# The last mixed pair of each chunk: three sums of weights on GpSimd in place of VectorE

## The chip, the cores and the metric

The kernel runs on one core of one Trainium2 chip. The metric is the device time of one execution in microseconds (us). Five engines share the core's on-chip memory: TensorE (PE in the rows, PEld for its weight loads), VectorE (DVE), ScalarE (ACT), GpSimd (POOL) and SyncE (SP), which issues the DMAs.

## The reference

One layer of an encoder, for 256 rows of width 2048, all in float32. Cut to what matters here:

```python
def swiglu(h, w_gate, w_up, w_down):
    return (jax.nn.silu(h @ w_gate) * (h @ w_up)) @ w_down

x = x + 0.5 * swiglu(rmsnorm(x, ffn1_norm), ffn1_w_gate, ffn1_w_up, ffn1_w_down)
...   # attention and linear attention, output product, cross attention on a memory
x = x + 0.5 * swiglu(rmsnorm(x, ffn2_norm), ffn2_w_gate, ffn2_w_up, ffn2_w_down)
```

The two SwiGLU stages (FFN 1 at the start, FFN 2 at the end) have weights of 2048x5632 (twice) and 5632x2048. They are the stages that the change touches.

## The kernel before, in words

**Split weights.** Every float32 weight tile is split in two on its way to TensorE: ScalarE rounds it to `wh` (a cast, L128), and VectorE computes the rest `wl` = weight minus `wh` (a subtraction, L129). Both are made in `parts`. A product is three matmuls: `wh` by the high part of the activations, `wl` by the same high part, and `wh` by the low part. `hth` and `htl` are the split activations of the first two products, `acth`/`actl` those of the third.

**Chunks.** An FFN runs in chunks. One call of `pair_gemm` is one chunk: for 512 columns of the gate and 512 of the up weight (11 chunks an FFN, c0 to c10), or for 1024 columns of the down weight (two calls after each group of 4, 4 and 3 chunks). So an FFN has 17 calls, and the kernel 34. A chunk goes over pairs of 128-row blocks of the weights, 8 pairs a chunk (6 in the last two down calls). A pair is one unit of the loop at L248 onward: DMA of a raw tile of 128x2048 (`raw`, 3 buffers), split, matmuls into four accumulators (`acc`).

**Plain and mixed pairs.** A plain pair has 24 matmuls of 512 columns. A mixed pair takes the 2x2 blocks of weights and activations by a scheme of seven products in place of eight, so it has 21 matmuls, but it wants four sums of weight blocks: `mixed_parts` (L203) makes t1 and t3 in one operation of 1024 columns (L208), then t2 (L213) and t4 (L214) of 512 columns each, into `wsum`, which has one buffer. t2 reads t1, and t4 reads t2. Then it splits three of the four raw blocks (1536 columns) and the four sums (2048 columns), each into a buffer of `wh` and one of `wl`; there are 4 buffers of each (`wspl`). Four of the seven products go into extra banks (`bank`), which `middle` (L302, L303) adds up after the last mixed pair.

**Order.** Pairs are taken in ORDER8 = (1, 0, 3, 2, 5, 4, 6, 7), with 1, 3 and 5 mixed, so that mixed and plain alternate; c0 of each FFN takes them in ORDER_FIRST = (0, 2, 4, 6, 1, 3, 5, 7), with the three mixed ones in a row. The 6-pair chunks take (1, 0, 3, 2, 4, 5) with 1 and 3 mixed. So a chunk's last mixed pair is pair 5, or pair 3 of six. Kernels of this kind give their operations in program order, and the framework's planner sets each engine's own queue when the program is built: at each moment of its own model it takes the operation that is ready and came first. On the chip each queue is then strictly in order. `issue_after(summed.ins)` tells the planner that the VectorE operations of the block (the two subtractions of L129) stand behind t4 in VectorE's queue.

**One mixed pair on the engines before:** VectorE makes the three sums, then the `wl` of the raw blocks; ScalarE casts the sums as soon as they and a buffer are there; then VectorE makes the `wl` of the sums. TensorE begins a mixed pair with the raw block B11 (three matmuls) and takes t1 next, `wh` first, then `wl`.

**GpSimd before** has a few small operations (the reciprocal square roots of L92 and L94 on 2 to 8 columns, constants) and the descriptors of some small DMAs of `setup_mix` (L436, L479 to L491).

Of the kernel before, what the change touches and what calls it, by code (L numbers as in the profile page):

```python
# [15 lines left out]
ALU = mybir.AluOpType  # L16
# [44 lines left out]
class Kernel:  # L61
# [138 lines left out]
            dma(raw[:, :, CW:], wb, cb, CW)  # L200
        return flat[:, :nk * 2 * CW]

    def mixed_parts(self, raw):  # L203
        nc = self.nc
        q = [raw[:, i * CW:(i + 1) * CW] for i in range(4)]
        t = self.wsum.tile([P, 4 * CW], F32, name="wsum")
        t1, t3, t2, t4 = (t[:, i * CW:(i + 1) * CW] for i in range(4))
        nc.vector.tensor_tensor(  # L208
            out=t[:, :2 * CW].rearrange("p (j n) -> p j n", j=2),
            in0=raw[:, CW:3 * CW].rearrange("p (j n) -> p j n", j=2),  # L210
            in1=q[0].unsqueeze(1).broadcast_to([P, 2, CW]), op=ALU.add,
        )
        nc.vector.tensor_tensor(out=t2, in0=t1, in1=q[2], op=ALU.add)  # L213
        summed = nc.vector.tensor_tensor(out=t4, in0=t2, in1=q[3], op=ALU.add)  # L214
        forms = {}
        with self.tc.issue_after(summed.ins):
            for src, names in ((raw[:, CW:], ("B11", "B22", "B21")), (t, ("t1", "t3", "t2", "t4"))):
                wh, wl = self.parts(src, 4 * CW)
                for i, name in enumerate(names):
                    forms[name] = tuple(w[:, i * CW:(i + 1) * CW] for w in (wh, wl))  # L220
        return forms

    def pair_gemm(self, xs, cols, k0, order, middle, ahead=None):

        nc = self.nc
        out = [[self.acc.tile([P, CW], F32, name="acc") for _ in range(2)] for _ in range(NB)]
        if ahead:
            ahead(0)  # L230

        units = []
        for p in order:
            units += [(p, (0,)), (p, (1,))] if ahead and not units else [(p, (0, 1))]
        mixed = [i for i, (p, _) in enumerate(units) if xs[p][0]]
        extra, seen = {}, set()
        side = self.pending
        self.pending = []

        def product(key, bank, high, part, stop):  # L240
            self.last_pe = nc.tensor.matmul(out=bank, lhsT=high, rhs=part, start=key not in seen, stop=stop)  # L241
            seen.add(key)

        def step(u):
            if side and not (mixed and mixed[0] <= u < mixed[-1]):
                side.pop(0)()

        for u, (p, kk) in enumerate(units):  # L248
            if ahead and u:
                ahead(u)  # L250
            last = u == len(units) - 1
            is_mixed, xh, xl = xs[p]
            with ExitStack() as first:
                if ahead and not u:
                    for ins in self.first:
                        first.enter_context(self.tc.issue_after(ins))
                raw = self.raw_pair(cols, k0 + 2 * p + kk[0], len(kk))
                if is_mixed:
                    forms = self.mixed_parts(raw)
                else:  # L260
                    wh, wl = self.parts(raw, 4 * CW)
            if is_mixed:
                if u == mixed[0]:
                    extra = {name: self.bank() for name in ("p1", "p5", "p7", "p6")}
                for name, i, form in self.MIXED:
                    key = self.PLACE.get(name, name)
                    bank = extra[name] if name in extra else out[key[0]][key[1]]
                    fh, fl = forms[form]
                    ah, al = (t[:, i * P:(i + 1) * P] for t in (xh, xl))
                    stop = u == mixed[-1] if name in extra else last  # L270
                    product(key, bank, ah, fh, False)
                    product(key, bank, ah, fl, False)
                    product(key, bank, al, fh, stop)
                if u == mixed[-1]:
                    middle(extra)
                    step(u)
                continue
            x = lambda t, k, b: t[:, (2 * k + b) * P:(2 * k + b + 1) * P]
            w = lambda t, k, c: t[:, (2 * (k - kk[0]) + c) * CW:(2 * (k - kk[0]) + c + 1) * CW]
            if last:  # L280

                turns = [(k, b, (c,)) for c in range(2) for b in range(NB) for k in kk]
            else:
                turns = [(k, b, (0, 1)) for k in kk for b in range(NB)]
            for t, (k, b, cs) in enumerate(turns):
                for c in cs:
                    product((b, c), out[b][c], x(xh, k, b), w(wh, k, c), False)
                    product((b, c), out[b][c], x(xh, k, b), w(wl, k, c), False)
                for c in cs:
                    product((b, c), out[b][c], x(xl, k, b), w(wh, k, c), last and k == kk[-1])  # L290
                if not last and b == NB - 1:
                    step(u)
        for piece in side:
            piece()
        return out

    def middle(self, extra):

        nc = self.nc
        p1, u3 = (self.sums.tile([P, CW], F32, name="su", bufs=4) for _ in range(2))  # L300
        u4, v = (self.sums.tile([P, CW], F32, name="sg", bufs=2) for _ in range(2))
        add = lambda out, a, b: nc.vector.tensor_tensor(out=out, in0=a, in1=b, op=ALU.add)  # L302
        nc.scalar.copy(out=p1, in_=extra["p1"])  # L303
        add(u4, extra["p6"], p1)
        add(u3, extra["p7"], u4)
        add(v, extra["p5"], u3)
        add(u4, extra["p5"], u4)
        return p1, u4, u3, v
# [897 lines left out]
```

## Time and profile before

| | |
|---|---|
| time, median of 3 runs | 1893.19 us (1891.2 to 1893.41) |
| profiled execution | 1893.06 us, of which the span of the trace 1891.4 us |
| mean granted TensorE clock | 0.995 |
| busy in the span | PE 98%, VectorE 82%, ScalarE 54%, GpSimd 3% |
| DMA | 56.2% of 16 engines' time, 187 GB/s read |

How to read it: a row of the timeline gives the start in us from the start of the span, the duration in us, engine, line, operation, what it writes and reads, the shapes, and in brackets the idle time of the engine before it with what ended that. A busy PE is not PE at its peak, since the ends of matmuls are modelled; the distance of the starts of two matmuls is what one costs (0.23 us for 512 columns at the full clock).

### The profile page before, as it was taken

How to read it: one execution, taken by the hardware profiler on the slowest of the kernel's cores; microseconds unless marked ns; L12 is line 12 of the kernel's file. 1: busy time of each engine (PE TensorE's matmuls, PEld its weight loads, DVE VectorE, ACT ScalarE, POOL GpSimd, SP SyncE). 2: the span in 40 equal slices, each digit the busy share in tenths (PEclk: the TensorE clock that was granted, in tenths of full speed). 3: DMA queues.
4: the chain of work that ended last, by engine and by line, in shares of the span. 5: the costliest groups of instructions: out<-in, count | busy, mean ns of one | idle time of the engine just before them, and what ended most of it. 6: DMA issues, size and time to landing. Idle time of an engine off the chain costs nothing.

```text
span 1891.4 us, 21793 instructions
## 1 busy us (share of the span) xinstructions
PE 1862.5 (98%) x8418; PEld 1529.6 (81%) x8418; DVE 1556.6 (82%) x1691; ACT 1017.2 (54%) x1088; POOL 60.7 (3%) x114
## 2 busy tenths in 40 slices
PE   8899999999999999999999999999999999999999
PEld 6688888888888888788778878778888888888887
DVE  7899999998999996555565645999998899999897
ACT  6555545555545554664555655655544555545552
POOL 1000000000000100120100020000000000000000
PEclk9899999999999999999999999999999999999999
DMA  7565556665566555544436553566556665556653
GB/s 247 178 201 200 183 200 213 193 205 198 201 212 201 188 183 178 174 156 146 133 133 210 178 169 133 178 200 200 201 197 204 204 198 200 199 200 201 200 200 134
DMA packets 148072, 356.01 MB, mean 188 GB/s; under 512 B 11018, under 2 KB 11120, under 8 KB 147968
## 3 DMA queue, kind: packets, MB, share of 16 engines
q1 hardware_dynamic: 147360, 354.07, 56.2%
q8 instruction: 66, 1.08, 0.2%
q0 software_dynamic: 608, 0.55, 0.2%
q14 instruction: 38, 0.31, 0.0%
HBM read 352.48 MB, written 2.10 MB: 187 GB/s over the span
## 4 chain that ended last, share of the span: by engine, by line
PE 92%; DVE 3%; ACT 3%; issue 1%; DMA 1%; POOL 0%; SPq 0%; ACTq 0%; DVEq 0%
PE acc L241 55%; PE acc L142 18%; PE bank L241 14%; PE bank L350 2%; ACT wh L128 1%; DVE wl L129 1%; ACT junk L384 1%; DMA raw<-in_ffn_w_up_dram 1%; DVE wsum L208 0%; PE bank L949 0%; PE bank L804 0%; PE bank L785 0%; PE bank L948 0%; PE bank L1003 0%; PE bank L1012 0%
## 5 line engine op out<-in xcount | busy, mean ns | idle before, releaser
L129 DVE TENSOR_TENSOR wl<-raw,wh 128x2048 fp32r<-128x2048 f32 (+4 forms) x405 | 716.4, 1771 | 192.1 <-ACT wh L128 190.9
L128 ACT CAST wh<-raw 128x2048 fp32r<-128x2048 f32 (+4 forms) x405 | 601.7, 1494 | 405.8 <-PE acc L241 172.0
L241 PE MATMUL acc<-wh,hth 128*128 128x512 f32 x1078 | 423.4, 395 | 4.2 <-ACT wh L128 4.2
L241 PE MATMUL acc<-wl,hth 128*128 128x512 f32 x1078 | 420.3, 390 | 0.8 <-DVE wl L129 0.8
L241 PE MATMUL acc<-wh,htl 128*128 128x512 f32 x1078 | 363.2, 390 | 0.0
L128 ACT CAST wh<-wsum 128x2048 fp32r<-128x2048 f32 x98 | 187.6, 1914 | 256.7 <-DVE wsum L214 182.5
L129 DVE TENSOR_TENSOR wl<-wsum,wh 128x2048 fp32r<-128x2048 f32 x98 | 224.5, 2291 | 39.6 <-ACT wh L128 39.6
L241 PEld LDWEIGHTS acc<-wh,hth 128*128 128x128 f32 x1078 | 203.4, 189 | 46.1 <-ACT wh L128 4.8
L241 PEld LDWEIGHTS acc<-wh,htl 128*128 128x128 f32 x1078 | 202.9, 188 | 42.9
L241 PEld LDWEIGHTS acc<-wl,hth 128*128 128x128 f32 x1078 | 203.0, 188 | 42.5 <-DVE wl L129 1.4
L241 PE MATMUL acc<-wh,actph 128*128 128x512 f32 x448 | 176.0, 393 | 0.0
L241 PE MATMUL acc<-wl,actph 128*128 128x512 f32 x448 | 174.4, 389 | 0.0
L241 PE MATMUL acc<-wh,actpl 128*128 128x512 f32 x448 | 145.6, 389 | 0.0
L208 DVE TENSOR_TENSOR wsum<-raw 128x1024 f32<-128x1024 f32 x98 | 119.5, 1219 | 3.8 <-DMA raw<-in_ffn_w_up_dram 2.2
L142 PE MATMUL acc<-wh,hth 128*128 128x512 f32 (+1 forms) x288 | 113.2, 395 | 0.0
L241 PE MATMUL bank<-wl,hth 128*128 128x512 f32 x264 | 105.8, 401 | 7.3 <-DVE wl L129 7.3
L142 PE MATMUL acc<-wl,hth 128*128 128x512 f32 (+1 forms) x288 | 109.9, 383 | 0.0
L241 PE MATMUL bank<-wh,hth 128*128 128x512 f32 x264 | 102.5, 396 | 3.6 <-ACT wh L128 3.6
L241 PE MATMUL bank<-wh,htl 128*128 128x512 f32 x264 | 104.4, 396 | 0.0
L241 PEld LDWEIGHTS acc<-wh,actpl 128*128 128x128 f32 x448 | 84.0, 188 | 17.9
L241 PEld LDWEIGHTS acc<-wh,actph 128*128 128x128 f32 x448 | 84.1, 188 | 17.1
L241 PEld LDWEIGHTS acc<-wl,actph 128*128 128x128 f32 x448 | 84.2, 188 | 16.9
(280 smaller groups left out, 2394.4 us busy)
## 6 DMA issues: line engine op xcount, KB each, us to landing
raw<-in_ffn_w_down_dram SPq DMA_DIRECT2D x88, 1024.0 KB, 5.0
raw<-in_ffn_w_gate_dram SPq DMA_DIRECT2D x175, 512.0 KB, 3.8
raw<-in_ffn_w_up_dram SPq DMA_DIRECT2D x175, 512.0 KB, 4.6
raw<-in_w_in_dram SPq DMA_DIRECT2D x24, 1024.0 KB, 5.0
raw<-in_w_out_dram SPq DMA_DIRECT2D x16, 1024.0 KB, 5.2
raw<-in_w_in_dram SPq DMA_DIRECT2D x8, 832.0 KB, 4.6
raw<-in_mem_w_k_dram SPq DMA_DIRECT2D x4, 1024.0 KB, 5.2
raw<-in_mem_w_q_dram SPq DMA_DIRECT2D x4, 1024.0 KB, 5.2
```

The lines of the kernel that those rows point to most:

```text
L128: self.last_act = nc.scalar.copy(out=wh, in_=src)
L129: self.last_dve = nc.vector.tensor_tensor(out=wl, in0=src, in1=wh.bitcast(F32), op=ALU.subtract)
L142: self.last_pe = nc.tensor.matmul(out=out[b][c][:, :w], lhsT=high, rhs=part[:, o:o + w], start=start, stop=stop)
L208: nc.vector.tensor_tensor(out=t[:, :2 * CW].rearrange("p (j n) -> p j n", j=2), in0=raw[:, CW:3 * CW].rearrange("p (j n) -> p j n", j=2), ...
L241: self.last_pe = nc.tensor.matmul(out=bank, lhsT=high, rhs=part, start=key not in seen, stop=stop)
L350: nc.tensor.transpose(out=t[:, i * P:(i + 1) * P], in_=src(b, k), identity=self.ident)
L384: self.nc.scalar.activation(out=junk[:, :width], in_=src, func=AF.Square, accum_out=out)
```

## The change

`mixed_parts` takes the engine for the three sums as an argument. For the last mixed pair of each call of `pair_gemm` it is GpSimd, for the others VectorE as before. Where it is GpSimd, the order edge that holds VectorE's subtractions behind the sums is left out. Of 98 mixed pairs 34 are the last of their call. Sizes, buffers, casts, subtractions, matmuls and DMAs stay.

```diff
-    def mixed_parts(self, raw):
-        nc = self.nc
+    def mixed_parts(self, raw, engine):
+
...
-        nc.vector.tensor_tensor(
+        engine.tensor_tensor(
             out=t[:, :2 * CW].rearrange("p (j n) -> p j n", j=2),
             in0=raw[:, CW:3 * CW].rearrange("p (j n) -> p j n", j=2),
             in1=q[0].unsqueeze(1).broadcast_to([P, 2, CW]), op=ALU.add,
         )
-        nc.vector.tensor_tensor(out=t2, in0=t1, in1=q[2], op=ALU.add)
-        summed = nc.vector.tensor_tensor(out=t4, in0=t2, in1=q[3], op=ALU.add)
+        engine.tensor_tensor(out=t2, in0=t1, in1=q[2], op=ALU.add)
+        summed = engine.tensor_tensor(out=t4, in0=t2, in1=q[3], op=ALU.add)
         forms = {}
-        with self.tc.issue_after(summed.ins):
+        with ExitStack() as order:
+            if engine is self.nc.vector:
+                order.enter_context(self.tc.issue_after(summed.ins))
...
-                    forms = self.mixed_parts(raw)
+                    forms = self.mixed_parts(raw, nc.gpsimd if u == mixed[-1] else nc.vector)
```

## Rows read from the trace of the kernel before

**Rows 1.** The page's busy times: us, share of the span, instructions.
```profile
PE 1862.5 (98%) x8418; PEld 1529.6 (81%) x8418; DVE 1556.6 (82%) x1691; ACT 1017.2 (54%) x1088; POOL 60.7 (3%) x114
```

**Rows 2.** What PE waited for: total us, times, longest us.
```profile
PE bank L241 <- DVE wl L129: 7.3, 3, 5.1
```

**Rows 3.** Busy times by stretch: us, PE, PEld, DVE, ACT, POOL; PEclk, DMA share, GB/s.
```profile
66.00:72.00 6.00, 4.93 (x11) 3.44 (x12) 5.63 (x4) 4.36 (x3) 0.00 (x0) 0.50 0.55 175
1231.00:1236.00 5.00, 5.00 (x12) 3.50 (x12) 5.00 (x4) 2.79 (x2) 0.00 (x0) 0.50 0.61 208
347.00:390.00 43.00, 43.00 (x196) 35.56 (x195) 39.40 (x38) 23.78 (x18) 0.00 (x0) 1.00 0.62 196
```

**Rows 4.** Timeline, FFN 1's chunk c6, its last mixed pair and the pair before it.
```profile
370.93 2.29 DVE L129 TENSOR_TENSOR wl<-wsum,wh 128x2048 fp32r<-128x2048 f32 x1 [0.40 <-ACT wh L128]
373.14 2.28 DVE L129 TENSOR_TENSOR wl<-raw,wh 128x2048 fp32r<-128x2048 f32 x1
375.34 1.22 DVE L208 TENSOR_TENSOR wsum<-raw 128x1024 f32<-128x1024 f32 x1
...
377.32 0.69 DVE L214 TENSOR_TENSOR wsum<-wsum,raw 128x512 f32<-128x512 f32 x1
377.93 1.75 DVE L129 TENSOR_TENSOR wl<-raw,wh 128x1536 fp32r<-128x1536 f32 x1
380.44 2.29 DVE L129 TENSOR_TENSOR wl<-wsum,wh 128x2048 fp32r<-128x2048 f32 x1 [0.76 <-ACT wh L128]
...
375.09 1.49 ACT L128 CAST wh<-raw 128x1536 fp32r<-128x1536 f32 x1 [2.39 <-issue]
378.49 1.92 ACT L128 CAST wh<-wsum 128x2048 fp32r<-128x2048 f32 x1 [1.92 <-PE acc L241]
...
385.95 0.39 PE L241 MATMUL bank<-wl,hth 128*128 128x512 f32 x1
```

**Rows 5.** Timeline: `wl` of sums and PE's t1, FFN 1's c1 and FFN 2's c10.
```profile
85.51 2.29 DVE L129 TENSOR_TENSOR wl<-wsum,wh 128x2048 fp32r<-128x2048 f32 x1 [0.40 <-ACT wh L128]
...
90.78 0.39 PE L241 MATMUL bank<-wl,hth 128*128 128x512 f32 x1
...
1796.80 2.29 DVE L129 TENSOR_TENSOR wl<-wsum,wh 128x2048 fp32r<-128x2048 f32 x1 [0.70 <-ACT wh L128]
...
1802.32 0.39 PE L241 MATMUL bank<-wl,hth 128*128 128x512 f32 x1
```

**Rows 6.** Timeline of GpSimd and VectorE: small GpSimd operations beside a subtraction, and alone.
```profile
840.65 1.30 POOL L92 TENSOR_SCALAR sm<-sm 128x4 f32<-128x4 f32 x1
...
840.69 1.21 DVE L129 TENSOR_TENSOR wl<-raw,wh 128x1024 fp32r<-128x1024 f32 x1
...
925.50 0.19 POOL L92 TENSOR_SCALAR sm<-sm 128x4 f32<-128x4 f32 x1
```

**Rows 7.** Groups of GpSimd instructions by form: busy us, mean ns of one, idle before.
```profile
L1034 POOL MEMSET zeros<- 128x256 f32 x1 | 0.3, 322 | 24.0 <-PE acc L142 24.0
...
L468 POOL TENSOR_SCALAR_AFFINE_SELECT suffix<-suffix 128x128 f32<-128x128 f32 x1 | 0.3, 307 | 0.0
...
masks.py:197 POOL MEMSET ident<- 128x128 f32 x1 | 0.2, 204 | 0.0
```

**Rows 8.** Timeline, the last mixed pair of c0: FFN 1, then FFN 2.
```profile
50.41 2.29 DVE L129 TENSOR_TENSOR wl<-wsum,wh 128x2048 fp32r<-128x2048 f32 x1 [0.35 <-ACT wh L128]
...
54.22 0.63 PE L241 MATMUL bank<-wl,hth 128*128 128x512 f32 x1
...
1216.90 2.29 DVE L129 TENSOR_TENSOR wl<-wsum,wh 128x2048 fp32r<-128x2048 f32 x1 [0.37 <-ACT wh L128]
...
1219.25 0.50 PE L241 MATMUL bank<-wl,hth 128*128 128x512 f32 x1
```

**Rows 9.** Timeline, the last mixed pair of FFN 1's last down call.
```profile
701.45 2.29 DVE L129 TENSOR_TENSOR wl<-wsum,wh 128x2048 fp32r<-128x2048 f32 x1 [0.37 <-ACT wh L128]
...
704.09 0.39 PE L241 MATMUL bank<-wl,actmh 128*128 128x512 f32 x1
```

## Prediction: what the change will do

> **What bounds the kernel now.** I read the page's busy times first, then the waits of TensorE, then the busy times by stretch, and last the timeline of single chunks. TensorE is busy for 98% of the span [rows 1]. In a stretch of 43 us of FFN 1 it is busy all of it at the full clock, while VectorE works 39.4 us and ScalarE 23.8 [rows 3]. So the two makers of split weights have slack there, and TensorE sets the pace. What TensorE loses to them in the FFNs lies at the starts: its waits for `wl` ahead of a bank come to 7.3 us in three places, 5.1 of them in one, on the first mixed pair after FFN 1's chunk c0 [rows 2]. Behind that wait, and behind the like one in FFN 2, the granted clock is 0.50, the lower level of 1.2 GHz, for some 5 us [rows 3].
>
> So taking work off VectorE can win only at the two starts. Everywhere else the question is whether the sums on GpSimd come in time.
>
> **What is removed.** For 34 pairs VectorE drops the three sums: from 375.34 to 378.01, 2.67 us each [rows 4], 91 us in all. In the steady chunks this is worth nothing, since TensorE doesn't wait there. The order edge that falls away lets VectorE make the raw part's `wl` as soon as its cast ends (375.09 + 1.49 = 376.58, instead of 377.93 [rows 4]); TensorE wants that part only at about 385, so that is worth nothing either. DMAs: none is added. A raw buffer comes free when the last sum has read it, some 2 us later than now, and the next transfer into it starts later; that load is for a pair two pairs ahead, some 11 us of matmuls (48 at 0.23), which covers it.
>
> **What one set of sums costs on GpSimd.** No row of the trace shows a wide addition there. Nearest are a fill of 256 columns at 322 ns and of 128 at 204, so 0.92 ns for each further element, and an operation that reads and writes 128 columns at 307 ns, so 0.8 ns per element for a read on top [rows 7]; a small operation alone takes 0.19 [rows 6]. The three sums are 2048 elements in three operations. Low end: one pass of 0.92 ns carries reads and write together, 1.9 + 3 x 0.19 = 2.45 us. High end: two reads and the write in turn, 0.92 + 2 x 0.8 = 2.5 ns an element, 5.7 us. I take 4.3: the two operands read in turn with the write beside them (2 x 0.92 ns, 3.8 + 0.57), near the middle of the ends. Below nothing is excluded, since the work does not vanish.
>
> The Trainium skill has a price: its page "GPSIMD Engine Reference", section "3.1 Elementwise — side-by-side cycle accounting", gives 4497 ns for one such addition of 2048 elements. By that the set would be about 4.6 us (an estimate, with 0.1 for two more starts), and the forecast below some 8 us higher. No run here shows it.
>
> **What it waits for.** `wsum` has one buffer, so GpSimd can't begin before VectorE has read the sums of the mixed pair before: at 373.22 in the chunk shown. VectorE goes on at once, at 373.14, with the plain pair's subtraction up to 375.42 [rows 4]. Beside such subtractions (two inputs from on-chip memory) GpSimd stands still: an operation that takes 0.19 us alone took 1.30 beside one, ending at 841.95, just behind VectorE's at 841.90, though it had begun 0.04 us earlier [rows 6]. So I let GpSimd begin at 375.4, where VectorE's own sums began too. Then VectorE's subtraction of the raw part, 1.75 us, falls due at 376.58, between GpSimd's operations, and one of the two waits. Either way the sums end later by that 1.75. With 0.3 us for three starts and hand-overs:
>
> later than now by 4.3 + 1.75 + 0.3 - 2.67 = 3.7 us (1.8 at the low end of 2.45, 5.1 at the high end).
>
> The skill's page "SBUF — State Buffer", section "Who interferes with whom", has this as a lock that whoever starts first keeps for its whole instruction. The row shows GpSimd waiting although it began first, so here the trace differs in that point; by the page it would be VectorE that waits at 376.58, with the same sum.
>
> **What covers it.** Behind the sums come ScalarE's cast and VectorE's subtraction of the sums; TensorE wants that `wl` at t1, its second product. In c6 the subtraction ends at 382.73 and TensorE takes it at 385.95: 3.2 us. Besides, the cast waits now 0.4 us longer than the sums need, for a buffer (378.49 against 378.01 and 0.1 for the hand-over) [rows 4]. Room 3.6. In the first of the steady chunks it is 90.78 - 87.80 = 3.0, in the last 3.2 and another 0.3 of waiting [rows 5]; over the 28 such pairs (34 less c0 and the two 6-pair calls of each FFN) it goes from 2.4 to 4.3, half of them under 3.4. What is over is a stall of TensorE, and not given back, because VectorE's lead is bound by buffers that TensorE frees. Summed over the 28 pairs with 3.7: 24 overrun, by 11 us in all, none by more than 1.3. At 1.8 none overruns; at 5.1 all do, 48 us.
>
> Queued behind the sums on GpSimd is next to nothing in the FFNs. VectorE's queue behind the waiting subtraction of the sums holds the next plain pair's, which TensorE wants 4.8 us later than t1 (21 matmuls), so that stays covered.
>
> **The places without that room.** In c0 of each FFN three mixed pairs follow one another. Room now: 54.22 - 52.70 = 1.5 in FFN 1, and 1219.25 - 1219.19, nothing, in FFN 2 [rows 8]; overruns 2.2 and 3.6. In FFN 1's last down call 704.09 - 703.74 = 0.35 [rows 9]; 3.3. The other three 6-pair calls have over 6 us of other VectorE work between the two sets, which GpSimd can use; I put nothing there. The stalls in FFN 2's c0 and in the down call are new and long; after such a wait the clock drops as above, and 5 us at 0.50 lose 2.5 each: 5.
>
> **Sum.** 11 + 2.2 + 3.6 + 3.3 + 5 = 25 us on the profiled 1893.06 (span 1891.4 and 1.7 around it), which is 0.1 below the median of the runs. Forecast 1918. With the low end 0 + 0.3 + 1.8 + 1.5 = 4 (1897, no wait over 2 us); with the high end 48 + 3.6 + 5.0 + 4.7 + 5 = 66 (1959).
>
> **Rivals.**
>
> *The starts get shorter (faster).* VectorE is busy 5.6 of 6 us and all of 5 us in the stretches about the two start waits [rows 3], and the sums of c0's last mixed pair stand 2.67 us ahead of them in its queue. If GpSimd makes these while VectorE does the raw part and the plain pair behind, and the planner lets TensorE take that plain pair first, each start gains up to 2.67, and FFN 1's another 2 us of waiting in c0 (7.3 less 5.1 [rows 2]): 7 us, 1886. It decides where the sums end no later than those two subtractions, 1.75 + 2.28 = 4 us after the buffer is free; with 4.3 and standing still they don't. It needs the steady pairs to be covered, too.
>
> *The cover holds.* If the sums cost under 3.3 us, or GpSimd isn't held for the whole of a subtraction, the 28 pairs overrun by nothing or next to it and only the starts and the down call are left: 0 to 8 us, 1893 to 1901.
>
> *Dearer, or in another order.* At the high end of the price all pairs overrun: up to 1959. The same comes if the planner, taking GpSimd for slow, puts the next plain pair's subtraction ahead of that of the sums on VectorE: 2.2 us more for each of 28 pairs, 62 less what room is left, again 1940 to 1970.
>
> That the change doesn't do what it says is excluded: each of the 34 calls has a last mixed pair, and the three sums are named by engine.
>
> **How the numbers follow.** A forecast like the sum (1902 to 1935): 0.50. The cover holds: 0.20, half of it within 0.2%. The starts get shorter: 0.12. Dearer: 0.18. 0.2%, 3.8 us, is about what a measurement of this kernel can tell from no change. Faster by more 0.12, within 0.11, slower by more 0.77. The range of 1889 to 1952 leaves out most of the faster case and the end of the dearest.
>
> **What would show it.** Right: GpSimd rows of L208, L213 and L214, 34 each, 4 to 5 us a set without waits and some 6 with the raw part's subtraction between; casts of the sums waiting for GpSimd in place of a buffer; TensorE waits of up to 1.3 us for `wl` at t1 in most chunks; lower clock in FFN 2's c0 and behind 704. Wrong: sets that end within 3 us of where VectorE's ended, no wait of TensorE in the steady chunks, or a shorter wait at about 66 and 1231.

## The result, and the profile after

| | before | after |
|---|---|---|
| time, median | 1893.3 us (4 runs, 1891.2 to 1893.4) | 1983.6 us (4 runs, 1982.9 to 1985.5) |
| profiled execution, its span | 1893.06, 1891.4 us | 1985.52, 1983.8 us |
| mean granted TensorE clock | 0.995 | 0.985 |
| busy: PE, VectorE, ScalarE, GpSimd | 98, 82, 54, 3% | 96, 77, 51, 17% |

After over before is 1.0481 (95% interval 1.0463 to 1.0499): 90 us slower. The forecast was 1918 with a range up to 1952. Right in its sign, it missed three quarters of the loss.

The page's busy times of after (us, share of the span, instructions), the counterpart of [rows 1]:

```profile
PE 1901.0 (96%) x8418; PEld 1539.9 (78%) x8418; DVE 1525.9 (77%) x1589; ACT 1010.5 (51%) x1088; POOL 335.9 (17%) x216
```

Waits of after (total us, times, longest us); the first line answers to [rows 2]:

```profile
PE bank L243 <- DVE wl L129: 48.0, 39, 4.4
PE bank L243 <- ACT wh L128: 14.0, 12, 4.8
...
DVE wsum L208 <- DMA raw<-in_ffn_w_up_dram: 33.9, 14, 2.8
DVE wsum L208 <- DMA raw<-in_ffn_w_down_dram: 15.0, 6, 2.9
```

Groups of after by form (busy us, mean ns of one, idle before them): the sums on GpSimd, and VectorE's subtraction of a mixed pair's raw blocks:

```profile
L208 POOL TENSOR_TENSOR wsum<-raw 128x1024 f32<-128x1024 f32 x34 | 145.1, 4267 | 1097.1 <-DVE wl L129 1097.0
...
L213 POOL TENSOR_TENSOR wsum<-wsum,raw 128x512 f32<-128x512 f32 x34 | 83.5, 2457 | 2.7
L214 POOL TENSOR_TENSOR wsum<-wsum,raw 128x512 f32<-128x512 f32 x34 | 46.8, 1376 | 2.7
L129 DVE TENSOR_TENSOR wl<-raw,wh 128x1536 fp32r<-128x1536 f32 x98 | 221.0, 2255 | 4.2 <-ACT wh L128 4.2
```

Three things stand out. TensorE's waits for `wl` grew from 3 to 39, but a single one is short. VectorE has less to do and yet its first sums wait 48.9 us for raw tiles, in 20 of the 34 calls; before, the wait ahead of them was under 4:

```profile
L208 DVE TENSOR_TENSOR wsum<-raw 128x1024 f32<-128x1024 f32 x98 | 119.5, 1219 | 3.8 <-DMA raw<-in_ffn_w_up_dram 2.2 <-DMA raw<-in_ffn_w_down_dram 0.6
```

And VectorE's subtraction of 1536 columns, 1.75 us in [rows 4], now takes 2.26 in the mean of all 98.

The timeline shows where that comes from. This is FFN 1's chunk c6 in after, from the moment when `wsum` is free to the same moment one chunk later: VectorE, then GpSimd, ScalarE, the transfers' queue and TensorE (start us, duration us, and in brackets the wait before it and what ended that). It answers to [rows 4].

```profile
394.21 2.29 DVE L129 TENSOR_TENSOR wl<-wsum,wh 128x2048 fp32r<-128x2048 f32 x1 [0.39 <-ACT wh L128]
...
398.62 3.96 DVE L129 TENSOR_TENSOR wl<-raw,wh 128x1536 fp32r<-128x1536 f32 x1
407.07 2.29 DVE L129 TENSOR_TENSOR wl<-wsum,wh 128x2048 fp32r<-128x2048 f32 x1 [4.50 <-ACT wh L128]
409.28 4.49 DVE L129 TENSOR_TENSOR wl<-raw,wh 128x2048 fp32r<-128x2048 f32 x2
413.69 0.68 DVE L304 TENSOR_TENSOR sg<-bank,su 128x512 f32<-128x512 f32 x1
416.76 1.23 DVE L208 TENSOR_TENSOR wsum<-raw 128x1024 f32<-128x1024 f32 x1 [2.40 <-DMA raw<-in_ffn_w_up_dram]
...
440.03 2.29 DVE L129 TENSOR_TENSOR wl<-wsum,wh 128x2048 fp32r<-128x2048 f32 x1 [0.39 <-ACT wh L128]
...
396.63 4.32 POOL L208 TENSOR_TENSOR wsum<-raw 128x1024 f32<-128x1024 f32 x1 [37.31 <-DVE wl L129]
401.03 2.70 POOL L213 TENSOR_TENSOR wsum<-wsum,raw 128x512 f32<-128x512 f32 x1
403.81 1.29 POOL L214 TENSOR_TENSOR wsum<-wsum,raw 128x512 f32<-128x512 f32 x1
...
405.13 1.91 ACT L128 CAST wh<-wsum 128x2048 fp32r<-128x2048 f32 x1 [6.70 <-POOL wsum L214]
...
411.59 0.37 SPq L193 DMA_DIRECT2D raw<-in_ffn_w_gate_dram  x1
412.00 0.47 SPq L193 DMA_DIRECT2D raw<-in_ffn_w_up_dram  x1
...
409.42 0.50 PE L243 MATMUL bank<-wl,hth 128*128 128x512 f32 x1 [1.45 <-DVE wl L129]
```

Follow the time from link to link. `wsum` is free at 396.50. The sums end at 405.10, 8.60 us later. ScalarE casts them; VectorE, which has had nothing to do since 402.57, begins their `wl` at 407.07 (1.97) and ends it at 409.36 (2.29). Behind it in VectorE's queue stands the plain pair's subtraction; when that has read its raw buffer, the transfer for the next chunk's first pair can be issued, at 411.59 (2.23). VectorE reads that tile at 416.76, having waited 2.40 us for it (5.17). Then it works almost without a pause, two mixed pairs and the end of the chunk before, until `wsum` is free again at 442.32 (25.56).

8.60 + 1.97 + 2.29 + 2.23 + 5.17 + 25.56 = 45.8 us, and that is the distance to the same point of the next chunk. The sum alone proves nothing, since it runs from one point to the same point; what makes it a loop is that the end of each link is what the next one waited or stood in the queue for. It closes without TensorE. The kernel before has it too, and its links stand in the trace of before: VectorE's first sums of the next chunk and the addition ahead of them, its `wl` that frees `wsum` for chunk c7, the issue of the transfer, and the DMA's share by stretch (us; PE, PEld, DVE, ACT, POOL; PEclk, DMA share, GB/s) while it lands.

```profile
389.44 0.68 DVE L302 TENSOR_TENSOR sg<-bank,su 128x512 f32<-128x512 f32 x1
390.09 1.23 DVE L208 TENSOR_TENSOR wsum<-raw 128x1024 f32<-128x1024 f32 x1
...
413.36 2.29 DVE L129 TENSOR_TENSOR wl<-wsum,wh 128x2048 fp32r<-128x2048 f32 x1 [0.38 <-ACT wh L128]
...
384.96 0.37 SPq L193 DMA_DIRECT2D raw<-in_ffn_w_gate_dram  x1
...
389.30:389.60 0.30, 0.30 (x3) 0.22 (x3) 0.30 (x2) 0.30 (x1) 0.00 (x0) 1.00 0.21 75
389.60:389.90 0.30, 0.30 (x3) 0.21 (x2) 0.30 (x1) 0.30 (x1) 0.00 (x0) 1.00 0.00 0
```

By these and [rows 4]: sums 4.79 us behind the free buffer, `wl` of the sums begun 2.43 later, 2.29 for it, 2.23 to the issue at 384.96, 5.13 to VectorE's first sums of the next chunk at 390.09, 25.56 to 415.65: 42.43 us, TensorE's own pace. Spare in it were about 0.4 us at the transfer, whose last bytes came before 389.6, and 0.4 at the cast, which waited for a buffer that TensorE frees. So the loop was some 0.8 us short of TensorE's 42.4 (an estimate from these two). The change made the first link longer by 3.81 and the second shorter by 0.46, the cast's spare. The transfer's spare did not help: its link is 5.17 us in after, with VectorE waiting at its end, against 5.13, so the transfer itself took longer there; no run asks why.

c6 is one of the dearer calls. From one t1 (TensorE's second product of the last mixed pair) to the next, 14 of the 28 steady calls took 3.2 to 3.9 us longer than in before, and the others 1.2 to 2.6, among them those behind a down call, where no first sums wait for a transfer. Together the 28 lost 74 us.

### The profile page after: what moved, and what is told of

The parts are those of the page before. It is cut to its first block, busy times and chain, and to the rows that moved or that the text cites. A ratio compares the mean times of both kernels' runs of the same rounds, so it can differ in the third digit from the quotient of the medians.

```text
span 1983.8 us, 21867 instructions
## 1 busy us (share of the span) xinstructions
PE 1901.0 (96%) x8418; PEld 1539.9 (78%) x8418; DVE 1525.9 (77%) x1589; ACT 1010.5 (51%) x1088; POOL 335.9 (17%) x216
## 4 chain that ended last, share of the span: by engine, by line
PE 30%; DVE 15%; POOL 7%; ACT 4%; issue 4%; DMA 2%; SPq 0%; DVEq 0%; ACTq 0%; POOLq 0%
PE acc L142 17%; DVE wl L129 8%; PE acc L243 7%; ACT wh L128 4%; POOL wsum L208 3%; DMA raw<-in_ffn_w_up_dram 2%; POOL wsum L213 2%; PE bank L243 2%; POOL wsum L214 1%; DVE wsum L214 1%; PE bank L352 1%; DVE wsum L213 1%; DVE sg L304 1%; DVE wsum L208 1%; DVE sg L582 1%
## 5 line engine op out<-in xcount | busy, mean ns | idle before, releaser
L129 DVE TENSOR_TENSOR wl<-raw,wh 128x2048 fp32r<-128x2048 f32 (+4 forms) x405 | 764.8, 1900 | 135.8 <-ACT wh L128 134.4
L243 PE MATMUL acc<-wh,hth 128*128 128x512 f32 x1078 | 427.7, 398 | 4.5 <-ACT wh L128 4.3
L208 POOL TENSOR_TENSOR wsum<-raw 128x1024 f32<-128x1024 f32 x34 | 145.1, 4267 | 1097.1 <-DVE wl L129 1097.0
L243 PE MATMUL bank<-wl,hth 128*128 128x512 f32 x264 | 112.1, 425 | 36.0 <-DVE wl L129 36.0
L243 PE MATMUL bank<-wh,hth 128*128 128x512 f32 x264 | 107.1, 413 | 13.2 <-ACT wh L128 13.2
L208 DVE TENSOR_TENSOR wsum<-raw 128x1024 f32<-128x1024 f32 x64 | 78.2, 1222 | 49.5 <-DMA raw<-in_ffn_w_up_dram 33.9
L243 PE MATMUL bank<-wh,htl 128*128 128x512 f32 x264 | 108.4, 411 | 0.0
```

The source lines that it names most:

```text
L129: self.last_dve = nc.vector.tensor_tensor(out=wl, in0=src, in1=wh.bitcast(F32), op=ALU.subtract)
L208: engine.tensor_tensor(out=t[:, :2 * CW].rearrange("p (j n) -> p j n", j=2), in0=raw[:, CW:3 * CW].rearrange("p (j n) -> p j n", j=2), in1 ...
```

## The experiments

Theories that the expectations name: *room* (my own: each late set of sums costs TensorE what is over its room, and no more), *raw* and *queue* (VectorE loses its lead to late transfers, or to the 4.5 us in which it stands), later joined in the *loop* above, *port* (VectorE and GpSimd take turns at the on-chip memory), and *order* (the planner's new order does it). Ratios are to the kernel before in the same session, with 95% intervals.

**Four runs against the order, the raw buffers and the queue.** The order alone, e_noedge: the sums stay on VectorE, and the last pair's edge goes.

```diff
-                    forms = self.mixed_parts(raw, nc.gpsimd if u == mixed[-1] else nc.vector)
+                    forms = self.mixed_parts(raw, nc.vector, u != mixed[-1])
...
-            if engine is self.nc.vector:
+            if edge:
```

> The sums of the last mixed pair stay on VectorE; only the order edge that holds VectorE's two subtractions behind them is left out for that pair. Order theory (the loss comes from the planner's other order once the edge is gone): most of the 90 us, above 1950. All theories in which GpSimd's late sums are the cause: 1893, within 4 us.

Measured 1894.9 us, ratio 1.0007 (0.9997 to 1.0017). VectorE now made the raw part's subtraction between its sums, which ended 6.3 us after the free buffer in place of 4.8, and TensorE didn't notice. The planner's order is not quite that of after here, though: behind c6 the next chunk's first sums stand six operations further back in VectorE's queue, at 396.53. The order theory falls by the trace of after itself: in 27 of the 34 calls, c6 among them, VectorE's queue is that of before without the three sums, operation for operation.

A fourth raw buffer, e_raw4:

```diff
+            self.wraw4 = pool("wraw4", 1)
...
-        flat = self.wraw.tile([P, 4 * CW], F32, name="raw")
+        self.turn = getattr(self, "turn", -1) + 1
+        flat = (self.wraw4 if self.turn % 4 == 3 else self.wraw).tile([P, 4 * CW], F32, name="raw")
```

> The change with a fourth raw buffer in the FFNs. To make room the low part of the activations of plain pairs goes into one spare tile that nothing reads, and TensorE reads the high part in its place (same matmuls). Raw theory (what costs the room is that the next chunk's first transfer can start only when the plain pair behind the late sums is split, so VectorE waits 2.4 us for it and its lead is gone): these waits go, the room before the sums is again some 3.6 us, and the time falls to about 1915 (1905 to 1930). Queue theory (VectorE's 4.5 us of standing for the sums' cast can't be made up, since it has some 3 us free in a chunk, whatever the buffers): 38.9 us of work and 4.5 of standing against 42.4 leave 1 us a chunk, and the time stays above 1925, with TensorE still waiting 1 us in each chunk. Room theory (each wait is a matter of its own pair): about 1983, no change.

(The rest of this edit makes room as the expectation says: what plain pairs leave out is the low part of their activations in the down products.)

One subtraction less for VectorE, e_light:

```diff
-                    wh, wl = self.parts(raw, 4 * CW)
+                    wh, wl = self.parts(raw, 4 * CW, last and not ahead)
...
         self.last_act = nc.scalar.copy(out=wh, in_=src)
+        if bare:
+            return wh, wh
```

> The change with VectorE spared one subtraction of 2.28 us in each call: the low part of the weights of the call's last plain pair is left out and the high part read in its place (same matmuls); calls with the first chunk's own order are as they were. Queue theory: 31 or 32 calls x 2.28 us, 60 to 70 us come back, about 1920. Raw theory: VectorE waits for the next chunk's transfer anyway, now 2.28 us longer, and the time stays at 1975 to 1985. Room theory: 1983.

Measured 1933.2 (1.0211, 1.0194 to 1.0228) and 1931.9 (1.0202, 1.0187 to 1.0217): either edit alone brings some 50 us back. Busy times from one free buffer to the next, chunk c6, in the run with four buffers and in the one with less work:

```profile
382.94:426.51 43.57, 42.96 (x193) 34.98 (x192) 37.72 (x35) 23.18 (x17) 8.29 (x3) 1.00 0.59 194
```

```profile
381.67:425.05 43.38, 43.04 (x194) 35.33 (x193) 35.50 (x33) 22.98 (x17) 8.31 (x3) 1.00 0.59 195
```

The loop explains both to 0.2 us: 45.80 less the 2.40 of waiting for the transfer is 43.40, and 45.80 less the 2.28 of the subtraction is 43.52. The raw theory was wrong that VectorE would merely wait longer for the transfer in the second: the wait stays (2.21 us), but the subtraction lies behind it in the loop. The room theory, with 1983 for both, falls. (The planner also moved some of VectorE's operations in these two runs, so the agreement is shown for c6 only.)

The buffer of the last mixed pair itself, e_rawearly:

```diff
-        engine.tensor_tensor(out=t2, in0=t1, in1=q[2], op=ALU.add)
-        summed = engine.tensor_tensor(out=t4, in0=t2, in1=q[3], op=ALU.add)
+        engine.tensor_tensor(out=t2, in0=t1, in1=t3 if engine is self.nc.gpsimd else q[2], op=ALU.add)
+        summed = engine.tensor_tensor(out=t4, in0=t2, in1=t3 if engine is self.nc.gpsimd else q[3], op=ALU.add)
```

> The change, but GpSimd's second and third sum read t3 in place of the raw blocks (so t2 and t4 are left out of the computation), which frees the raw buffer of the last mixed pair after VectorE's subtraction, some 2.5 us earlier. If it is this buffer that holds back the transfers: 1983 less 28 x 2, about 1925. If it is the buffer of the plain pair behind, whose subtraction stands behind that of the sums: 1975 to 1985, and the transfer for the next chunk's first pair starts as late as before.

Measured 1983.0 (1.0473, 1.0452 to 1.0494), as the change. The transfer into the buffer that GpSimd's sums hold was issued 6.1 us after `wsum` was free in place of 8.6, and the next chunk's first one as late as in after, at 15.1. So this buffer is not the one: it is the plain pair's, whose subtraction stands behind theirs.

**What GpSimd does to VectorE.** e_dup leaves the kernel before as it is and only lets GpSimd make the same sums beside it:

```diff
+        if twice:
+            self.adds(nc.gpsimd, raw, self.wtwo.tile([P, 4 * CW], F32, name="wtwo"))
```

> The kernel before, VectorE's sums and order edge as they were; GpSimd makes the same three sums of each last mixed pair a second time, into a tile that nothing reads (room for it by the spare tile, as in the run with four raw buffers). Nobody waits for GpSimd's result, only the raw buffer for its last read. Port theory (of VectorE and GpSimd only one gets at the on-chip memory at a time, for a whole instruction): VectorE's 38.9 us a chunk grow by GpSimd's 5.0 to 43.9 against 42.4, 1.5 us or more a chunk, 1935 to 1965, and VectorE's subtractions of 1.75 and 2.28 us stretch by up to 2.4. Without a shared port: 1893 to 1900 with the durations as before.

Measured 1993.7 (1.0531, 1.0510 to 1.0552): more than the change itself, though nobody waits for GpSimd's results. (It doesn't hold the raw buffer longest either: its last read ends at 447.30, VectorE's own at 450.25.) VectorE and GpSimd about chunk c7's last mixed pair, and busy times from the `wl` of c6's sums to that of c7's:

```profile
443.85 2.31 DVE L206 TENSOR_TENSOR wsum<-raw 128x1024 f32<-128x1024 f32 x1
446.19 1.67 DVE L211 TENSOR_TENSOR wsum<-wsum,raw 128x512 f32<-128x512 f32 x1
...
437.88 3.89 POOL L206 TENSOR_TENSOR wtwo<-raw 128x1024 f32<-128x1024 f32 x1 [38.08 <-DMA raw<-in_ffn_w_up_dram]
441.86 3.22 POOL L211 TENSOR_TENSOR wtwo<-wtwo,raw 128x512 f32<-128x512 f32 x1
445.15 2.15 POOL L212 TENSOR_TENSOR wtwo<-wtwo,raw 128x512 f32<-128x512 f32 x1
...
406.70:452.90 46.20, 43.94 (x195) 35.27 (x193) 43.03 (x37) 23.44 (x18) 9.26 (x3) 1.00 0.55 182
```

VectorE's first sums take 2.31 us in place of 1.22, its second 1.67 in place of 0.69, and they end 9.1 us after the free buffer in place of 4.8. The port theory holds, its number didn't: I had added GpSimd's 5.0 us to VectorE's work and forgotten the wait for the transfer, 2.26 us here, that the lateness brings. From 406.7 to 452.9 VectorE is busy for 43.0 of 46.2 us, 4.1 more than the expectation's 38.9; the rest is this wait and some 0.8 us of waits for casts.

The same turns are in after's c6 above. GpSimd's first sum stands from 396.63 until VectorE's plain subtraction ends, about 398.6, then runs to 400.95, 2.33 us; VectorE's subtraction, begun 398.62, stands through it and needs another 1.62; GpSimd's second stands through that. The Trainium skill, "SBUF — State Buffer", section "Who interferes with whom", says that VectorE instructions with two on-chip inputs contend with GpSimd instructions that read, and that who issues first keeps the shared ports for its whole instruction. On the whole instruction this trace agrees, with 3.96 us for a subtraction of 1.75. On who goes first it does not always: in c5 GpSimd's sum had begun 2 us before VectorE's second subtraction and stood through that too (last section).

**Starting GpSimd earlier**, e_wsum2 (with room made as for the fourth raw buffer):

```diff
-            self.wsum, ... = pool("wsum", 1), ...
+            self.wsum, ... = pool("wsum", 2), ...
```

> The change with two buffers for the sums (same spare tile to make room), so GpSimd can begin when the raw tile has landed. Loop theory (a loop of sums, cast, subtractions, freed raw buffer, transfer and VectorE's work of the next pairs, 45.8 us long, has taken over from TensorE's 42.4): the sums end earlier by the wait for the buffer, and as VectorE's and GpSimd's work together, 36.2 + 5.0 us, is under 42.4, the loop falls back below TensorE's: 1893 to 1915. If GpSimd's standing behind VectorE keeps the sums as late as now: 1960 to 1983.

Measured 1944.8 (1.0275, 1.0258 to 1.0292), between the two. GpSimd began up to 5 us sooner in the steady chunks, and in 12 of the 34 calls the sums ended 4.4 us, not 8.6, after the point where the single buffer would have been free; but what it took came out of VectorE, as the mean of its subtractions shows (2048 columns; [rows 4] has 2.28 and 2.29):

```profile
L129 DVE TENSOR_TENSOR wl<-raw,wh 128x2048 fp32r<-128x2048 f32 x165 | 399.5, 2430 | 19.0 <-ACT wh L128 19.0
L129 DVE TENSOR_TENSOR wl<-wsum,wh 128x2048 fp32r<-128x2048 f32 x98 | 249.2, 2542 | 101.8 <-ACT wh L128 101.8
```

VectorE also kept 37.1 us of waiting for raw tiles. Adding up the two engines' work, as the expectation did, leaves such waits out.

**More room at TensorE**, e_bfirst:

```diff
-                for name, i, form in self.MIXED:
+                for name, i, form in [self.MIXED[j] for j in ((0, 5, 6, 1, 2, 3, 4) if u else range(7))]:
```

> The change, but TensorE takes the three products with raw blocks (p1, p2, p3) of a mixed pair first and t1 fourth, in all mixed pairs but the first of a chunk: six matmuls, 1.36 us, more room for the sums. Room theory (TensorE waits because the sums come too late for their place): 28 x 1.36 = 38 us less, about 1945. Loop theory (TensorE is not in the loop that sets the pace): 1975 to 1985, the waits only shift.

Measured 1964.9 (1.0379, 1.0364 to 1.0395), between the theories. From c6 to c7 the buffer comes free 45.3 us later (392.21 to 437.47), against 45.8: six matmuls of room gave 0.5 us. But the planner had also put the next chunk's first sums behind other work of VectorE. The wait for their tile reaches VectorE all the same, through ScalarE: its cast of that tile waits 3.96 us for the transfer, a cast for the activations stands behind it, and VectorE waits 1.72 for that one. So this run does not settle its own size. With all sums on VectorE the same order (b_bfirst, the control) does nothing:

> The kernel before, all sums on VectorE, with the products of raw blocks first as in the run that gave the sums 1.36 us more room. TensorE waits at three places, 7.3 us in all, and 5.1 of them lie at a chunk's first mixed pair, which keeps its order: at most 2 us less, 1890 to 1895 by all theories.

Measured 1892.9, 0.9994 (0.9985 to 1.0004).

**A smaller dose**, e_t4only:

```diff
-        engine.tensor_tensor(out=t2, in0=t1, in1=q[2], op=ALU.add)
+        self.nc.vector.tensor_tensor(out=t2, in0=t1, in1=q[2], op=ALU.add)
```

(and the first sum likewise; the third stays with the argument's engine.)

> Only the third sum (t4, 512 columns) of the last mixed pair on GpSimd, the first two on VectorE, without the order edge. Loop theory: 0.6 us more of work for the two together and at most one subtraction of 1.75 in between, sums later by 0.6 to 2.4 us, which stays under the room and under TensorE's 42.4: 1893 to 1900. If the loss goes with the share of the work on GpSimd (a quarter of the columns): 1915.

Measured 1903.9 (1.0057, 1.0037 to 1.0077). In the steady chunks TensorE keeps its pace: behind c6 the buffer comes free 42.12 us later (376.35 to 418.47), though the sums end 7.1 us after it was free. That is as late as in e_edge below, which loses some 2 us in such a chunk, so the run is no test of the loop as it stands in after: the planner has put the next chunk's first sums six operations further back here, as in e_noedge, and they come when their tile has long landed (VectorE, then ScalarE's cast of that tile).

```profile
397.59 1.22 DVE L208 TENSOR_TENSOR wsum<-raw 128x1024 f32<-128x1024 f32 x1
...
395.07 1.48 ACT L128 CAST wh<-raw 128x1536 fp32r<-128x1536 f32 x1 [1.80 <-DMA raw<-in_ffn_w_up_dram]
```

So the place of these sums in VectorE's queue is itself a part of the loop. Moving them alone, with all three late sums on GpSimd, was not tried. What the run costs lies at the starts and at the last down calls of the FFNs, which the expectation had left out.

**The edge put back**, e_edge: VectorE's raw subtraction waits for GpSimd's third sum.

```diff
+                if engine is self.nc.gpsimd and src is not t:
+                    self.tc.add_manual_dep(self.last_dve.ins, summed.ins.name, ...Sync...)
```

> The change, with VectorE's subtraction of the raw part of the last mixed pair made to wait for GpSimd's third sum, as it stood behind the sums before; VectorE's queue is otherwise that of the change. Port theory (VectorE and GpSimd take turns at the on-chip memory, so this subtraction only pushes GpSimd's sums back; standing behind them it would fill the time of ScalarE's cast instead): the sums end 6.9 us after their buffer is free in place of 8.6, the loop shrinks from 45.8 to 44.1 us a chunk, and the time falls by some 1.7 x 29 = 50, to about 1933 (1925 to 1945). If the edge that fell away is worth nothing, as the prediction had it: 1980 to 1986.

Measured 1938.4 (1.0234, 1.0219 to 1.0250): 45 us of the 90 come back by making VectorE wait. Chunk c6:

```profile
390.93 1.76 DVE L129 TENSOR_TENSOR wl<-raw,wh 128x1536 fp32r<-128x1536 f32 x1 [5.02 <-POOL wsum L214]
392.88 2.29 DVE L129 TENSOR_TENSOR wl<-wsum,wh 128x2048 fp32r<-128x2048 f32 x1 [0.19 <-ACT wh L128]
...
402.62 1.23 DVE L208 TENSOR_TENSOR wsum<-raw 128x1024 f32<-128x1024 f32 x1 [2.44 <-DMA raw<-in_ffn_w_up_dram]
...
383.84 4.32 POOL L208 TENSOR_TENSOR wsum<-raw 128x1024 f32<-128x1024 f32 x1 [37.22 <-DVE wl L129]
388.24 1.29 POOL L213 TENSOR_TENSOR wsum<-wsum,raw 128x512 f32<-128x512 f32 x1
389.61 1.29 POOL L214 TENSOR_TENSOR wsum<-wsum,raw 128x512 f32<-128x512 f32 x1
```

The second sum is 1.29 us again, the sums end 7.19 us after the free buffer, and the subtraction of 1.76 fills the time of ScalarE's cast (0.19 us of waiting in place of 4.50). The loop is 44.5 us; the wait for the transfer, 2.44, is still in it.

**Edge and fourth buffer together**, e_edge_raw4, and the control b_raw4, the kernel before with the fourth buffer:

> The same wait and the fourth raw buffer together (spare tile as before). If what is left of the loop after the fourth buffer (1.1 us a chunk) is the unfilled time of the cast, VectorE's and GpSimd's work with the cast hidden comes under TensorE's 42.4 us and the steady chunks cost nothing any more; the starts (some 12 us with four buffers) stay: 1900 to 1915. If the 1.1 us have another cause: 1925 to 1935, as with four buffers alone.

> Control: the kernel before with the fourth raw buffer and the spare tile, all sums on VectorE. Steady chunks are set by TensorE, so all theories: 1889 to 1896. Over 1900 would say that the way room was made costs something itself.

Measured 1911.7 (1.0095, 1.0080 to 1.0110) and 1895.0 (1.0006, 0.9996 to 1.0016). Chunk c6 of the first:

```profile
376.40:419.00 42.60, 42.60 (x194) 35.28 (x193) 36.49 (x34) 23.29 (x17) 6.91 (x3) 1.00 0.62 198
```

TensorE is busy throughout, at 42.4 us a chunk by its own marks: with both links taken out of the loop the sums on GpSimd cost the steady chunks next to nothing (3.6 us in the 28). The 18 us that are left lie at c0 of FFN 1 (3.0), at FFN 1's last down calls (7.6), at c0 of FFN 2 (4.8) and in small pieces; they were not followed further. No version beat the kernel before.

## Why the prediction was wrong, step by step

- **What bounds the kernel.** That TensorE sets the pace was right. That "the two makers of split weights have slack there" was read from busy times, 39.4 of 43 us [rows 3], and was wrong in effect: VectorE's 3.6 free us lie in waits inside a loop whose own length was some 0.8 us short of TensorE's. This is the step that failed. In the sum it is the term of 11 us for the 28 steady pairs: they cost 74, measured from t1 to t1.
- **"The next transfer into it starts later ... which covers it."** The buffer I looked at, the last mixed pair's, was indeed covered (e_rawearly). I didn't ask it of the plain pair's buffer behind it, which waits as long as VectorE's queue does. That one cost 50 us (e_raw4).
- **"VectorE's lead is bound by buffers that TensorE frees."** For the cast that was so in before [rows 4]. In after, the buffer that decides is a raw one, which VectorE frees itself, and the 24 overruns of 11 us in all became 39 waits of 48, the starts' among them. So the room of 3.6 us, measured on a chunk that starts with its full lead, was not there in the next: c6 shows 1.45 us of waiting where 0.2 were due.
- **"The order edge ... is worth nothing."** True with all sums on VectorE (e_noedge, +0.07%, no change within its interval), but 45 us with GpSimd (e_edge). I had allowed for the 1.75 us by which the subtraction pushes back the sums, but not for the time of the cast that it had filled; "on TensorE's side it is wanted only later" was the wrong question.
- **The price of the sums.** 4.3 us forecast; 2.41 us for 1024 columns where no subtraction of VectorE's holds it up (GpSimd's timeline in FFN 2's last down call, below) and 1.29 for 512 twice make 5.0, inside the bounds. Nothing of the miss lies here: the sums end 8.60 - 4.79 = 3.8 us later in c6, and I had 3.7. The Trainium skill's figure ("GPSIMD Engine Reference", section "3.1 Elementwise — side-by-side cycle accounting"), by which I had estimated 4.6, was nearer than the bounds' middle.

```profile
1945.83 2.41 POOL L208 TENSOR_TENSOR wsum<-raw 128x1024 f32<-128x1024 f32 x1 [25.04 <-DVE wl L129]
```

- **Who stands behind whom.** GpSimd waits for the plain subtraction first, as forecast. My doubt of the lock, from the start times of [rows 6], was half borne out: who has the memory keeps it for a whole instruction, on either side (398.62, 443.85), but the one that starts first is not always the one that has it (c5, last section).
- **The starts.** By t1, FFN 1's c0 lost 3.8 (2.2 forecast), FFN 1's last down call 1.4 (3.3), and the stretch from there to FFN 2's c0 7.3 (3.6, and 5 of clock for these two): 12.5 in all for a forecast of 14.1. Close in sum, with some luck in the parts. The 6-pair calls for which the forecast had nothing lost 5.5, most of it in the one before FFN 1's last.
- **The clock.** I charged 5 us for stretches at the lower level. After has more of them: in the FFNs some 115 matmuls start 0.4 to 0.5 us apart, against some 30 in before. In the steady chunks no cost of their own shows, as a loop without TensorE would have it: t1 of c6 starts at 409.42, and t1 of the next two calls (first and last line), with busy times of a stretch between them at a granted clock of 0.50, stand as below. The call without such a stretch takes 45.8 us, the one with it, seven slow matmuls, 45.6.

```profile
455.23 0.50 PE L243 MATMUL bank<-wl,hth 128*128 128x512 f32 x1 [1.83 <-DVE wl L129]
...
458.30:460.00 1.70, 1.70 (x6) 1.31 (x5) 1.70 (x2) 0.80 (x1) 0.00 (x0) 0.50 0.67 198
...
500.82 0.50 PE L243 MATMUL bank<-wl,actmh 128*128 128x512 f32 x1 [1.23 <-DVE wl L129]
```

- **The rivals.** None was it. "Dearer, or in another order" gave 1940 to 1970, near the truth in size, but through a price or an order of VectorE's queue that didn't come.

## What to carry to other kernels

Room from a producer to its consumer is only half of what covers a delay: also follow the loop from the delayed work through the buffer that it frees, the transfer that waits for this buffer, and the producer's own queue, and compare its length with the consumer's pace. Follow it in the order that the planner gave: in e_t4only, where the next chunk's first sums stood further back, sums 2.3 us later than in before cost the steady chunks nothing. A busy share of 90% can mean that there is no slack at all. And work moved from VectorE to GpSimd is not taken off VectorE where VectorE's operations take two inputs from on-chip memory: count it as VectorE's own time at up to GpSimd's duration (4.1 of 5.0 us in e_dup), and keep something of VectorE's to do while the next engine works on the result.

## What was not expected of the hardware

- VectorE stood while GpSimd's instruction ran: a subtraction of 1.75 us took 3.96 when GpSimd's 1024-column sum had begun before it, and VectorE's 0.69 us sum 1.67. Idle GpSimd cycles were not free cycles: the same sums made in vain cost 100 us (e_dup).
- The turns need not alternate. In the timeline of after, chunk c5, GpSimd's first sum took 5.99 us: it stood through both of VectorE's subtractions, which together took their usual time, though the second began 2 us after it (350.39 + 3.95 - 1.75 = 352.59).

```profile
350.60 5.99 POOL L208 TENSOR_TENSOR wsum<-raw 128x1024 f32<-128x1024 f32 x1 [35.05 <-DVE wl L129]
...
350.39 3.95 DVE L129 TENSOR_TENSOR wl<-raw,wh 128x2048 fp32r<-128x2048 f32 x2
```
